# A hand-written TensorE order for the attentions of a second block: slots of one head and two query blocks, with pieces of projections between

## The chip, the cores and the metric

The kernel runs on one core of one Trainium2 chip. The metric is the device time of one execution in microseconds (us), the median over runs.

## The reference

Two blocks follow each other on a sequence of 512 tokens with 1024 features, in fp32. The first (a state-space branch and a windowed attention, then a feed-forward part) is left as it is. The change lies in the second block:

```python
z = rms_norm(x, g_norm) @ w_in
q, k, v, fl, gf, u, gs, qm, gm, gl = split_cols(z)
# forgetting attention: 12 heads of 64, causal, in 4 query blocks of 128
s = q.k/sqrt(64) + F_t - F_s          # F = cumsum(log_sigmoid(fl + b))
y_fox = softmax(s) @ v * silu(gf)
# S5: 48 groups of 16 channels, complex diagonal states; then gelu and a gated unit
y_s5 = gelu(s5_ssm(u)); y_s5 = y_s5 * sigmoid(y_s5 @ w_glu + b_glu) * silu(gs)
# memory attention: 4 heads of 128 over 256 memory keys
y_mem = softmax(qm.mk/sqrt(128)) @ mv * silu(gm)
merged = sum of sigmoid(gl_b) * (y_b @ w_proj_b) over the three branches
```

## The kernel before

Every projection is three products in a reduced fp32 format (hi times hi, hi times lo, lo times hi): `load_w` (L214) loads 512 KB of weights into `raw` (three buffers), ScalarE copies them to `whi` (L183) and VectorE writes the rest to `wlo` (L186); `whi` and `wlo` have two buffers each. `mm3` (L222) issues the three products of one 128-row slice, so a projection (`proj2`) is 24 matmuls of 512 columns into one of three PSUM banks, and a gated unit's second projection (`dense` on `w_glu`) 18.

The stretch that the change touches has ten units of work. Six are `fox(i)`, a pair of heads each: the projections of k, q and the gate; for each head the scores of query blocks 0 and 3 and then of 1 and 2 (tile `s`, two PSUM buffers), each with a row maximum (L782), its negative (L784), the exponential on ScalarE (tile `p`), a reciprocal (L795) and a scaling (L797), all in `softmax_rows`; then transposes of the scaled blocks on TensorE into the one PSUM bank of `pT`, five per two query blocks, in a group of four and a single one, each copied by ScalarE into `pt`; then 20 products with the values into `y`. Four are `mem(h)`, a memory head each. Beside them run the slots of S5 (`s5_slots`): per slot 8 products `px`, a scan and a dozen VectorE operations on them, 16 products `py`, a gelu, and small DMAs from GpSimd's queue (`ub`, `yp`). After S5 come six `glu(m)`, each the gate projection GS and the gated unit's projection.

A scheduling layer orders every engine's instructions: it simulates the program and, among instructions that are ready, takes the one of the highest priority, which follows the order of the text but for `tc.high_priority`. So TensorE's order is the scheduler's: single matmuls of projections of the next pairs stand between scores, transposes and S5 products. At run time each engine takes its instructions strictly in the order so fixed.

```python
ins[0]()
for x in range(10):
    if x < 9:
        ins[x + 1]()
    with tc.high_priority(offset=400):
        work[x]()
    next(s5_slot, None)
```

Of the kernel before, what the change touches and what calls it, by code (L numbers as in the profile page):

```python
# [8 lines left out]
F32 = mybir.dt.float32  # L9
# [8 lines left out]
P = 128  # L18
# [138 lines left out]
def emit(ctx, tc, A, out):  # L157
# [19 lines left out]
    set_banks(3)  # L177
    ctx.callback(lambda: banks["s"].close())

    V, S, G, T, DMA, QS = nc.vector, nc.scalar, nc.gpsimd, nc.tensor, nc.sync, nc.gpsimd  # L180
# [63 lines left out]
    def split(hi, lo, v):  # L244
        return act(hi, v, AF.Copy), tt(lo, v, f(hi), SUB)
# [1274 lines left out]
    def rtile(nm):  # L1520
        return qp.tile([P, L], F32, tag="r", name=nm, bufs=2)
# [38 lines left out]
    def fox_in(i):  # L1560
        a = proj2(U_K + i)
        kk = rtile("kk")
        act(kk, a, AF.Copy)
        kh = qp.tile([P, 2, L], F32R, tag="kh", name="kh", bufs=2)
        kl = kls[i % 2]
        for j in range(2):
            src = kk[64 * j:64 * j + 64]
            for q0 in (0, 64):
                act(kh[q0:q0 + 64, j], src, AF.Copy)
            tt(kl[64 * j:64 * j + 64, j], src, f(kh[64 * j:64 * j + 64, j]), SUB)  # L1570
        a = proj2(U_Q + i)
        r = rtile("r")
        act(r, a, AF.Copy, scale=0.125)
        f_in[i] = (kh, kl, split_heads(qp, r))

    def fox(i):
        kh, kl, qq = f_in.pop(i)
        pts = {}
        for hh in range(2):
            h = 2 * i + hh  # L1580
            lh = qp.tile([P, L], F32R, tag="lh", name="lh", bufs=2)
            h0, o0 = 64 * hh, 64 - 64 * hh
            G.tensor_copy(lh[h0:h0 + 64], qq[h0:h0 + 64, hh])
            V.tensor_scalar(lh[o0:o0 + 64], f(lf[o0:o0 + 64]), col("fsel", h)[o0:o0 + 64], None, op0=MUL)

            def score(n, hh=hh, lh=lh):
                sc = ps.tile([P, 512], F32, tag="s", name="s", bufs=2)
                w = max(256, (n + 1) * P)
                ql = qq[:, hh, n * P:(n + 1) * P]
                T.matmul(sc[:, 0:w], lhsT=ql, rhs=kh[:, hh, 0:w], start=True, stop=False)  # L1590
                T.matmul(sc[:, 0:w], lhsT=lh[:, n * P:(n + 1) * P], rhs=kl[:, hh, 0:w], start=False, stop=False)
                T.matmul(sc[:, n * P:(n + 1) * P], lhsT=identb, rhs=le_b, start=False, stop=True)  # L1592
                return sc[:, 0:(n + 1) * P]
            for ns in ((0, 3), (1, 2)):
                pr = softmax_rows([lambda n=n: score(n) for n in ns], None, qp, 512, 4)
                bl_ = [(n, kb) for n in ns for kb in range(n + 1)]
                pt = transposed([pr[ns.index(n)][:, kb * P:(kb + 1) * P] for n, kb in bl_], qp, 5, 4)
                for x, (n, kb) in enumerate(bl_):
                    pts[hh, n, kb] = pt[:, x]
        py = ps.tile([P, 512], F32, tag="y", name="y", bufs=1)  # L1600
        with tc.high_priority(offset=1000):
            for n in (2, 1, 3, 0):
                for kb in range(n, -1, -1):
                    for hh in (1, 0):
                        mm = T.matmul(py[64 * hh:64 * hh + 64, n * P:(n + 1) * P],
                                      lhsT=vx[:, kb, (2 * i + hh) * 64:(2 * i + hh) * 64 + 64],
                                      rhs=pts[hh, n, kb], start=(kb == n), stop=(kb == 0)).ins
                        in_order(mm, first=(n == 2 and kb == 2 and hh == 1))
        a = proj2(U_GF + i)
        s = rtile("sgf")  # L1610
        gate2(a, s)
        stt(yf[:, i], s, 0.5, py, MUL, MUL)


    ym = []

    def mem_in(h):
        a = proj2(U_QM + h)
        r = rtile("r")
        act(r, a, AF.Copy, scale=float(128.0 ** -0.5))  # L1620
        qq = qp.tile([P, 2, L], F32R, tag="qq", name="qm", bufs=2)
        split(qq[:, 0], qq[:, 1], r)
        f_in["m", h] = qq

    def mem(h):
        qq = f_in.pop(("m", h))
# [6 lines left out]
        pts = {}  # L1633
        for n2 in range(2):
            pr = softmax_rows([lambda n=n: score(n) for n in (2 * n2, 2 * n2 + 1)], None, qp, 512, 4)
            pt = transposed([pr[j][:, kb * P:(kb + 1) * P] for kb in range(2) for j in range(2)], qp, 5, 4)
            for kb in range(2):
                pts[n2, kb] = pt[:, 2 * kb:2 * kb + 2].rearrange("p a b -> p (a b)")
        py = ps.tile([P, 512], F32, tag="y", name="y", bufs=1)
        for n2 in range(2):  # L1640
            for kb in range(2):
                T.matmul(py[:, 256 * n2:256 * n2 + 256], lhsT=mvx[:, kb, h * P:(h + 1) * P], rhs=pts[n2, kb],
                         start=(kb == 0), stop=(kb == 1))
        a = proj2(U_GM + h)
        s = rtile("sgm")
        gate2(a, s)
        ym.append(pkv.tile([P, L], F32, tag=f"mk{h}", name=f"ym{h}"))
        stt(ym[h], s, 0.5, py, MUL, MUL)
# [32 lines left out]
    ins = [lambda i=i: fox_in(i) for i in range(6)] + [lambda h=h: mem_in(h) for h in range(4)]  # L1681
    work = [lambda i=i: fox(i) for i in range(6)] + [lambda h=h: mem(h) for h in range(4)]
    GLU = {5: (0,), 6: (1,), 7: (2, 3), 8: (4,), 9: (5,)}
    ins[0]()
    for x in range(10):
        if x < 9:
            ins[x + 1]()
        with tc.high_priority(offset=400):
            work[x]()
        next(s5_slot, None)  # L1690
        if x == 4:
            run(s5_slot)
            glu_in()
        for m in GLU.get(x, ()):
            glu(m)
# [134 lines left out]
```

## Time and profile before

| | |
|---|---|
| median of 3 runs | 2029.27 us (2028.99 to 2034.67) |
| the profiled execution's own time | 2029.36 us |
| its span on the core | 2027.6 us |
| TensorE busy | 1958.2 us, 97% of the span |
| VectorE busy | 1344.9 us, 66% |
| ScalarE busy | 967.5 us, 48% |
| chain that ended last | TensorE 89%, VectorE 5%, ScalarE 3% |

The span runs from the first instruction's start to the last one's end; the execution's own time has 1.8 us around it. Busy time of TensorE counts a matmul from issue to its modelled end, so a matmul of 512 columns has 0.39 us in the record although the next starts 0.23 us after it. PE is TensorE, DVE VectorE, ACT ScalarE, POOL GpSimd, SP the engine that issues the weights' DMAs.

### The profile page before, as it was taken

To read this page: it belongs to the slowest core of one execution; us is meant where nothing else is said; L and a number is where in the kernel's file an instruction comes from. 1 tells how busy PE (TensorE), PEld (TensorE's weight loads), DVE (VectorE), ACT (ScalarE), POOL (GpSimd) and SP (SyncE) were. 2 spreads that over 40 slices of the span, in tenths; PEclk is the share of its full clock that TensorE was granted. 3 is DMA by queue.
4 is the path that set the end of the run, shared out by engine and by line. 5 is a ranking of instruction groups with operands and counts; after the bars stand their busy time and mean duration, and the time that the engine had idled before them with its cause. 6 is when DMAs were issued, how large, how long until landed. Compare 5 with 4: busy or idle time off the path is not lost.

```text
span 2027.6 us, 29457 instructions
## 1 busy us (share of the span) xinstructions
PE 1958.2 (97%) x11312; PEld 1612.4 (80%) x11312; DVE 1344.9 (66%) x2375; ACT 967.5 (48%) x1825; POOL 214.2 (11%) x354
## 2 busy tenths in 40 slices
PE   6998999999999899999999999999999899999998
PEld 4787888888888777778777878878988677888887
DVE  6878877879567766457988885573587655524344
ACT  6745555454246665335433244554465644423233
POOL 2111111102020000001001210000532100000000
PEclk9998999999999999999999999999999999999999
DMA  7443545545322022343354643345764121333332
GB/s 297 116 146 125 158 140 178 182 129 170 94 63 63 22 84 88 100 125 110 116 169 128 218 145 97 105 123 167 193 178 130 47 66 58 135 96 88 104 97 90
DMA packets 84667, 250.48 MB, mean 124 GB/s; under 512 B 11632, under 2 KB 23280, under 8 KB 83760
## 3 DMA queue, kind: packets, MB, share of 16 engines
q1 hardware_dynamic: 67376, 199.45, 31.9%
q0 software_dynamic: 17152, 49.17, 7.8%
q8 instruction: 89, 1.46, 0.3%
q14 instruction: 50, 0.41, 0.1%
HBM read 228.78 MB, written 16.65 MB: 121 GB/s over the span
## 4 chain that ended last, share of the span: by engine, by line
PE 89%; DVE 5%; ACT 3%; DMA 1%; issue 1%; POOL 1%; SPq 0%; DVEq 0%; ACTq 0%; POOLq 0%
PE p L223 6%; PE p L225 6%; PE p L224 6%; PE pl L223 5%; PE pl L225 5%; PE pl L224 5%; PE po L223 3%; PE po L224 3%; PE po L225 3%; PE y L659 2%; PE pT L807 2%; PE ub L225 2%; PE pdn L225 2%; PE ua L225 2%; PE pdn L223 2%; PE ub L223 2%
## 5 line engine op out<-in xcount | busy, mean ns | idle before, releaser
L186 DVE TENSOR_TENSOR wlo<-raw,whi 128x1024 fp32r<-128x1024 f32 (+3 forms) x283 | 329.1, 1164 | 275.0 <-ACT whi L183 268.6
L183 ACT ACTIVATE whi<-raw 128x1024 fp32r<-128x1024 f32 (+3 forms) x283 | 282.8, 1001 | 445.3 <-PE p L224 135.0
L223 PE MATMUL pl<-hl,whi 128*128 128x512 f32 x528 | 212.5, 403 | 10.7 <-DVE cvc L189 8.2
L225 PE MATMUL pl<-hl,wlo 128*128 128x512 f32 x528 | 210.6, 399 | 1.0 <-DVE wlo L186 1.0
L224 PE MATMUL pl<-hl,whi 128*128 128x512 f32 x528 | 210.4, 398 | 0.0
L223 PE MATMUL p<-h,whi 128*128 128x512 f32 x504 | 200.2, 399 | 1.9 <-ACT uf L183 0.8
L225 PE MATMUL p<-h,wlo 128*128 128x512 f32 x504 | 199.7, 397 | 1.1 <-DVE wlo L186 1.1
L224 PE MATMUL p<-h,whi 128*128 128x512 f32 x504 | 199.6, 396 | 0.0
L223 PEld LDWEIGHTS pl<-hl,whi 128*128 128x128 f32 x528 | 100.8, 191 | 29.0 <-issue 10.4
L225 PEld LDWEIGHTS pl<-hl,wlo 128*128 128x128 f32 x528 | 100.6, 190 | 23.6 <-DVE wlo L186 1.7
L183 ACT ACTIVATE p<-s,nm 128x512 f32<-128x512 f32 (+4 forms) x128 | 80.1, 627 | 74.0 <-PE pT L807 34.2
L223 PEld LDWEIGHTS p<-h,whi 128*128 128x128 f32 x504 | 95.3, 189 | 22.9 <-ACT uf L183 1.2
L225 PEld LDWEIGHTS p<-h,wlo 128*128 128x128 f32 x504 | 95.1, 189 | 22.2 <-DVE wlo L186 2.0
L782 DVE TENSOR_REDUCE nm<-s 128x1 f32<-128x512 f32 (+4 forms) x128 | 76.6, 610 | 53.9 <-PE s L1592 28.7
L224 PEld LDWEIGHTS pl<-hl,whi 128*128 128x128 f32 x528 | 100.7, 191 | 13.8
L224 PEld LDWEIGHTS p<-h,whi 128*128 128x128 f32 x504 | 95.1, 189 | 20.1 <-DVE h L186 0.3
L183 ACT ACTIVATE pt<-pT 128x512 f32<-128x512 f32 (+1 forms) x152 | 70.7, 478 | 64.7 <-PE pT L807 52.8
L183 ACT ACTIVATE inj<-cs_t,dwt 128x128 f32<-128x128 f32 x256 | 80.9, 393 | 34.7 <-DVE es L635 27.7
L807 PE MATMUL pT<-cs_t,p 128*128 128x128 f32 x440 | 73.5, 281 | 9.9 <-ACT pt L183 9.6
L640 POOL DMA_DIRECT2D cf<-rows x64 | 34.7, 548 | 349.0 <-PE y L659 345.0
L225 PE MATMUL ua<-hf,wlo 128*128 128x512 f32 x176 | 69.4, 394 | 0.7 <-DVE wlo L186 0.7
L225 PE MATMUL ub<-hf,wlo 128*128 128x512 f32 x176 | 70.0, 398 | 0.0
(543 smaller groups left out, 4757.5 us busy)
## 6 DMA issues: line engine op xcount, KB each, us to landing
raw<-in_w_ta SPq DMA_DIRECT2D x66, 512.0 KB, 3.6
raw<-in_w_tb SPq DMA_DIRECT2D x63, 512.0 KB, 3.6
raw<-in_w_up SPq DMA_DIRECT2D x44, 512.0 KB, 3.6
es<-rows POOLq DMA_DIRECT2D x64, 256.0 KB, 5.7
cf<-rows POOLq DMA_DIRECT2D x64, 256.0 KB, 4.9
raw<-in_w_mod SPq DMA_DIRECT2D x32, 512.0 KB, 3.8
raw<-in_w_os SPq DMA_DIRECT2D x16, 512.0 KB, 3.8
raw<-in_w_out SPq DMA_DIRECT2D x16, 512.0 KB, 3.6
```

The costliest lines, as they stand in the source:

```text
L183: return S.activation(o, i, f, **kw)
L186: return eng.tensor_tensor(o, a, b, op=op)
L223: T.matmul(ps, lhsT=wh, rhs=ah, start=first, stop=False)
L224: T.matmul(ps, lhsT=wh, rhs=al, start=False, stop=False)
L225: T.matmul(ps, lhsT=wl, rhs=ah, start=False, stop=last)
L640: QS.dma_start(out=c_, in_=rows[r, 1].partition_broadcast(P))
L659: mm = T.matmul(py[64 * j:64 * j + 64, sl], lhsT=lt, rhs=rh, start=(step == 2), stop=(step == 0)).ins
L782: V.tensor_reduce(nm[:, j:j + 1], src, axis=AX.X, op=MAX)
L807: T.transpose(pt[:, j * P:(j + 1) * P], b, ident)
```

## The change

All products go through a class that, once switched on, ties each to the one before it, so that in this stretch TensorE's order is the order of the text. Projections are generators that yield after 12 of 24 matmuls. The text is a loop over pairs x, with four slots for a pair of heads and two for a memory head; a slot holds the scores of one head's two query blocks, four transposes of the slot before, 12 matmuls of a projection, the fifth transpose, and in some slots 12 more. Values and gate of a pair come a pair later. The order of the other engines is still the scheduler's. All counts of instructions, their shapes and all buffers stay.

```diff
+    class Products:
+        on, last = False, None
+        def put(self, r):
+            if self.on:
+                if self.last is not None:
+                    tc.add_manual_dep(r.ins, self.last.name, mybir.DependencyInfo(
+                        mybir.DependencyClass.NoSync, mybir.DependencyReason.DATA), reason="order")
+                self.last = r.ins
+            return r
...
+    def half_proj2(t, consume):
+        a = bank("p2")
+        hi, lo = load_w(flat(A["w_tb"][t]))
+        for k in range(KD):
+            ks = slice(k * P, (k + 1) * P)
+            mm3(a, hi[:, ks], lo[:, ks], acth[0](k), acth[1](k), k == 0, k == KD - 1)
+            if k == KD // 2 - 1:
+                yield
+        consume(a)
+        yield
...
     def glu(m):
-        a = proj2(U_GS + m)
-        gate2(a, s)
+        yield from half_proj2(U_GS + m, lambda a: gate2(a, s))
         pg = bank("pg")
         dense(flat(A["w_glu"][m]), 6, [act5], [pg])
...
+    run(fox_q(0))
+    run(fox_k(0))
+    T.on = True
+    for x in range(11):
+        slots = 4 if x < 6 else 2 if x < 10 else 1
+        qn = fox_q(x + 1) if x < 5 else mem_q(x - 5) if x < 9 else nothing()
+        kn = fox_k(x + 1) if x < 5 else nothing()
+        for s_ in range(slots):
+            if x < 6:
+                pr = fox_scores(x, s_ // 2, NS2[s_ % 2])
+            elif x < 10:
+                pr = mem_scores(x - 6, s_)
+            if s_ == 1:
...
+                    gate = gate_of(U_GF + x - 1 if x < 7 else U_GM + x - 7, o_, py_)
+            if turning:
+                step(turning)
+            if s_ == 0:
+                step(qn)
+            elif s_ == 1:
+                step(qn)
+            elif s_ == 2:
+                step(kn)
+            else:
+                step(gate)
+            if turning:
+                run(turning)
+            if x < 6:
+                if s_ == 1:
+                    step(kn)
...
+                elif s_ == 2:
+                    step(gate)
+            elif s_ == 1:
+                step(gate, 2)
+            else:
+                step(glus, 3)
+            if x < 10:
+                turning = turned(pr, pts_[x])
+            if x == 10:
+                step(glus, 6)
+        if x < 5:
+            fox_lh(2 * x + 2)
+            next(s5_slot, None)
+            if x == 4:
+                run(s5_slot)
+                glu_in()
+        if x == 5:
+            glus = (y for m in range(6) for y in glu(m))
+            step(glus, 3)
+        elif 5 < x < 10:
+            step(glus, 1 if x == 7 else 0)
```

**First pair, TensorE.** Before, from the S5 products `px` on: `p_13556` and `p_13596` are projections of the next pair, `s` the scores (L1590 to L1592).

```order
L1462 MATMUL px_13437<-ub,w_13270 128x64 x8
L225 MATMUL p_13556<-h_12445,wlo 128x512
L223 MATMUL p_13556<-h_12445,whi 128x512
L1590 MATMUL s<-kh,qq 128x256
L1590 MATMUL s<-kh,qq 128x512
L224 MATMUL p_13556<-h_12445,whi 128x512
L225 MATMUL p_13556<-h_12445,wlo 128x512
L223 MATMUL p_13556<-h_12445,whi 128x512
```

Now (every matmul carries the class's line, L195); `p_13583` is q of the next pair, of which 12 matmuls stand ahead of these rows, and `pT` are the transposes of the first slot's blocks:

```order
L195 MATMUL s<-kh,qq 128x256
L195 MATMUL s<-kl_12838,lh 128x256
L195 LDWEIGHTS cbf
L195 MATMUL s<-cbf 128x128
L195 MATMUL s<-kh,qq 128x384
L195 MATMUL s<-kl_12838,lh 128x384
L195 LDWEIGHTS cbf
L195 MATMUL s<-cbf 128x128
L198 MATMUL pT<-cs_t,p 128x128 x4
L195 MATMUL p_13583<-h_12445,whi 128x512 x2
```

Before, two projections and more of a third stood between the first scores and their completion; now the first slot's transposes come 12 matmuls and one slot's scores after them.

**First pair, VectorE.** Before, the work behind the first maxima (L782); `t_13822`, `uf` are the gelu of S5, `qq` a split of q:

```order
L186 TENSOR_TENSOR hs<-gr,xw_13455 128x8x64
L782 TENSOR_REDUCE nm<-s 128x1 x2
L186 TENSOR_TENSOR wlo<-raw,whi 128x1024
L186 TENSOR_TENSOR t_13822<-t_13822,yv 128x512
L784 TENSOR_SCALAR nm<-nm 128x1
L186 TENSOR_TENSOR qq<-r,qq 64x512
L784 TENSOR_SCALAR nm<-nm 128x1
L186 TENSOR_TENSOR qq<-r,qq 64x512
L189 SCALAR_TENSOR_TENSOR uf<-t_13822,yv 128x512
L795 RECIPROCAL sm<-sm 128x2
L797 TENSOR_SCALAR p<-p,sm 128x128
L797 TENSOR_SCALAR p<-p,sm 128x512
```

Now, up to the same two scalings (L817); the first maximum stands five rows further up, L802 is the maximum, L815 the reciprocal, `xr`, `xw` and `gr` (the scan) are S5's:

```order
L206 TENSOR_TENSOR xw<-xw,e_13271 128x512
L804 TENSOR_SCALAR nm<-nm 128x1
L206 TENSOR_TENSOR xr<-xr,xw 128x512
L802 TENSOR_REDUCE nm<-s 128x1
L1488 SCALAR_TENSOR_TENSOR gr<-e_13271,xr 128x512
L815 RECIPROCAL sm<-sm 128x2
L804 TENSOR_SCALAR nm<-nm 128x1
L1619 TENSOR_SCALAR lh<-lf,cols 64x512
L802 TENSOR_REDUCE nm<-s 128x1
L1461 COPY up<-uf 128x512
L817 TENSOR_SCALAR p<-p,sm 128x128
L817 TENSOR_SCALAR p<-p,sm 128x512
```

Before, the S5 operations up to `hs` lay ahead of the first maximum; now the S5 chain of that slot and the maxima of the next slot lie between the first maximum and the scalings.

**Gated units, ScalarE.** Before, `whi` of a gated unit (768 columns) stands with that of the gate ahead of it, six rows before the gate is used (`sg_15636`):

```order
L183 ACTIVATE whi<-raw 128x1024
L183 ACTIVATE whi<-raw 128x768
L183 ACTIVATE p,sm<-s,nm 128x128
L183 ACTIVATE pt<-pT 128x512
L183 ACTIVATE p,sm<-s,nm 128x512
L183 ACTIVATE pt<-pT 128x128
L183 ACTIVATE whi<-raw 128x1024
L183 ACTIVATE sg_15636<-p_15605 128x512
```

Now, for the gated unit m=1 (gate `p_15457`):

```order
L203 ACTIVATE p,sm<-s,nm 128x256 x2
L203 ACTIVATE pt<-pT 128x128
L203 ACTIVATE whi<-raw 128x768
L203 ACTIVATE sg_15456<-p_15457 128x512
L203 ACTIVATE whi<-raw 128x1024
L203 ACTIVATE t_15515<-pg,hb 128x512
```

The gated unit's `whi` now stands right ahead of the use of the gate's projection, with which it shares a buffer: a memory head's q projection is half done on TensorE and holds the other. In the built program two adjacent loads share their buffer in this way five times: m=1 behind its gate, m=2 behind its gate, m=3 behind its gate, the gate of m=4 behind m=3, and the gate of memory head 1 behind the q of memory head 3. Before, there is no such place.

## Rows read from the trace of the kernel before

**Rows 1.** The page: span, and busy time of each engine.

```profile
span 2027.6 us, 29457 instructions
PE 1958.2 (97%) x11312; PEld 1612.4 (80%) x11312; DVE 1344.9 (66%) x2375; ACT 967.5 (48%) x1825; POOL 214.2 (11%) x354
```

**Rows 2.** Busy time in three stretches: us, then PE, PEld, DVE, ACT, POOL, clock, DMA.

```profile
1450.00:1560.00 110.00, 110.00 (x651) 93.37 (x650) 87.12 (x163) 70.07 (x133) 40.05 (x71) 1.00 0.63 170
1560.00:1700.00 140.00, 128.86 (x793) 104.73 (x792) 81.52 (x189) 71.70 (x166) 10.12 (x13) 0.99 0.21 59
1700.00:1757.00 57.00, 57.00 (x276) 47.67 (x275) 29.36 (x61) 23.73 (x47) 0.00 (x0) 1.00 0.25 74
```

**Rows 3.** Who TensorE waited for, 1560 to 1700: us, times, longest.

```profile
PE pT L807 <- ACT pt L183: 6.7, 3, 2.8
PE y L1605 <- ACT pt L183: 2.2, 3, 1.1
```

**Rows 4.** Timeline of the longest wait: start, duration, engine, operation.

```profile
1577.08 2.56 ACT L183 ACTIVATE kh<-kk 64x512 fp32r<-64x512 f32 x4
...
1577.86 0.28 PE L807 MATMUL pT<-cs_t,p 128*128 128x128 f32 x1
...
1579.66 1.06 ACT L183 ACTIVATE whi<-raw 128x1024 fp32r<-128x1024 f32 x1
...
1580.62 0.26 ACT L183 ACTIVATE pt<-pT 128x128 f32<-128x128 f32 x1
...
1580.94 0.66 PE L807 MATMUL pT<-cs_t,p 128*128 128x128 f32 x4 [2.80 <-ACT pt L183]
```

**Rows 5.** Stretches around another wait, columns as in rows 2 (clock third from the end).

```profile
1606.00:1610.00 4.00, 1.44 (x10) 1.08 (x9) 2.91 (x8) 3.93 (x8) 0.82 (x1) 1.00 0.00 0
1610.00:1614.00 4.00, 4.00 (x13) 2.79 (x12) 3.24 (x8) 2.75 (x8) 0.00 (x0) 0.57 0.42 131
```

**Rows 6.** Timeline of TensorE: two projection matmuls, a pair's values; chain: S5's `px`.

```profile
1560.02 0.39 PE L224 MATMUL p<-h,whi 128*128 128x512 f32 x1
1560.25 0.39 PE L225 MATMUL p<-h,wlo 128*128 128x512 f32 x1
...
1565.05 2.40 PE L1605 MATMUL y<-pt,vx 128*64 128x128 f32 x40
...
1467.25 1.73 PE px L1462 x16
```

**Rows 7.** A stretch with S5 beside the attention, columns as in rows 2.

```profile
1500.00:1520.00 20.00, 20.00 (x115) 16.87 (x114) 17.46 (x37) 13.75 (x29) 7.01 (x13) 1.00 0.57 174
```

**Rows 8.** Timeline of VectorE: two operations, one behind the other.

```profile
1502.99 0.67 DVE L1441 COPY up<-uf 128x512 f32<-128x512 f32 x1
1503.59 1.14 DVE L189 SCALAR_TENSOR_TENSOR yv<-uf,cols,yp 128x512 f32<-128x512 f32 x1
```

**Rows 9.** Groups by line and form, 1450 to 1760: count, busy us, mean ns, idle before.

```profile
L186 DVE TENSOR_TENSOR wlo<-raw,whi 128x1024 fp32r<-128x1024 f32 x32 | 39.1, 1222 | 17.5 <-ACT whi L183 16.8 <-DMA w<-s5k 0.3
L183 ACT ACTIVATE whi<-raw 128x1024 fp32r<-128x1024 f32 x32 | 33.9, 1058 | 35.1 <-PE p L224 22.2 <-issue 9.5 <-PE pg L224 3.3
L186 DVE TENSOR_TENSOR wlo<-raw,whi 128x768 fp32r<-128x768 f32 x7 | 6.7, 953 | 7.8 <-ACT whi L183 7.8
L183 ACT ACTIVATE whi<-raw 128x768 fp32r<-128x768 f32 x7 | 5.9, 841 | 6.1 <-PE p L224 4.8 <-PE pg L224 1.3
L183 ACT ACTIVATE kh<-kk 64x512 fp32r<-64x512 f32 x24 | 15.1, 630 | 1.1 <-PE s L1590 0.8
L183 ACT ACTIVATE kk<-p 128x512 f32<-128x512 f32 x6 | 3.5, 590 | 0.0
L183 ACT ACTIVATE pt<-pT 128x512 f32<-128x512 f32 x32 | 19.1, 596 | 13.0 <-PE pT L807 13.0
L183 ACT ACTIVATE p<-s,nm 128x256 f32<-128x256 f32 x28 | 13.2, 472 | 29.7 <-PE pT L807 20.4 <-DVE nm L784 7.5 <-PE s L1592 1.5
```

More of the change, by code (lines that the diff above doesn't have):

```diff
@@ L178, in emit, with matmul, transpose @@
     ctx.callback(lambda: banks["s"].close())
-    V, S, G, T, DMA, QS = nc.vector, nc.scalar, nc.gpsimd, nc.tensor, nc.sync, nc.gpsimd
+    V, S, G, DMA, QS = nc.vector, nc.scalar, nc.gpsimd, nc.sync, nc.gpsimd
+    class Products:
[7 more added lines that the diff above has]
+            return r
+        def matmul(self, *a, **k):
+            return self.put(nc.tensor.matmul(*a, **k))
+        def transpose(self, *a, **k):
+            return self.put(nc.tensor.transpose(*a, **k))
+    T = Products()
     def act(o, i, f, **kw):
@@ L1558, in emit @@
     f_in = {}
[L1560 to L1599, printed above, removed]
-        py = ps.tile([P, 512], F32, tag="y", name="y", bufs=1)
[L1601 to L1610, printed above, removed]
-        gate2(a, s)
-        stt(yf[:, i], s, 0.5, py, MUL, MUL)
@@ L1615, in emit @@
-    ym = []
[L1617 to L1626, printed above, removed]
+    def half_proj2(t, consume):
[8 more added lines that the diff above has]
+        yield
@@ new lines, in fox_q, with consume, fox_k @@
+    def fox_q(i):
+        def consume(a):
+            r = rtile("r")
+            act(r, a, AF.Copy, scale=0.125)
+            f_in["q", i] = split_heads(qp, r)
+        return half_proj2(U_Q + i, consume)
+    def fox_k(i):
+        def consume(a):
+            kk = rtile("kk")
+            act(kk, a, AF.Copy)
+            kh = qp.tile([P, 2, L], F32R, tag="kh", name="kh", bufs=2)
+            kl = kls[i % 2]
+            for j in range(2):
+                src = kk[64 * j:64 * j + 64]
+                for q0 in (0, 64):
+                    act(kh[q0:q0 + 64, j], src, AF.Copy)
+                tt(kl[64 * j:64 * j + 64, j], src, f(kh[64 * j:64 * j + 64, j]), SUB)
+            f_in["k", i] = kh, kl
+        return half_proj2(U_K + i, consume)
@@ new lines, in turned @@
+    def turned(blocks, pts):
+        o = qp.tile([P, 5, P], F32, tag="pt", name="pt", bufs=4)
+        for x0 in range(0, len(blocks), 4):
+            pt = pst("pT")
+            bs = blocks[x0:x0 + 4]
+            for x, (key, b) in enumerate(bs):
+                T.transpose(pt[:, x * P:(x + 1) * P], b, ident)
+                pts[key] = o[:, x0 + x]
+            act(o[:, x0:x0 + len(bs)], v3(pt[:, 0:len(bs) * P], len(bs)), AF.Copy)
+            yield
+        pts["tile", blocks[0][0]] = o
@@ new lines, in fox_values, with gate_of, consume @@
+    def fox_values(i, pts):
+        py = ps.tile([P, 512], F32, tag="y", name="y", bufs=1)
+        for n in (0, 3, 1, 2):
+            for kb in range(n + 1):
+                for hh in range(2):
+                    T.matmul(py[64 * hh:64 * hh + 64, n * P:(n + 1) * P],
+                             lhsT=vx[:, kb, (2 * i + hh) * 64:(2 * i + hh) * 64 + 64],
+                             rhs=pts[hh, n, kb], start=(kb == 0), stop=(kb == n))
+        return py
+    def gate_of(t, o, py):
+        def consume(a):
+            s = rtile("sg")
+            gate2(a, s)
+            stt(o, s, 0.5, py, MUL, MUL)
+        return half_proj2(t, consume)
@@ L1628, in score, with mem_q, consume, mem_scores @@
+    ym = []
+    def mem_q(h):
+        def consume(a):
+            r = rtile("r")
+            act(r, a, AF.Copy, scale=float(128.0 ** -0.5))
+            qq = qp.tile([P, 2, L], F32R, tag="qq", name="qm", bufs=2)
+            split(qq[:, 0], qq[:, 1], r)
+            f_in["m", h] = qq
+        return half_proj2(U_QM + h, consume)
+    def mem_scores(h, n2):
+        qq = f_in["m", h]
         def score(n):
@@ L1632, in score, with mem_values @@
             return sc[:, 0:256]
[L1633 to L1638, printed above, removed]
+        pr = softmax_rows([lambda n=n: score(n) for n in (2 * n2, 2 * n2 + 1)], None, qp, 512, 4)
+        return [((n2, kb, j), pr[j][:, kb * P:(kb + 1) * P]) for kb in range(2) for j in range(2)]
+    def mem_values(h, pts):
         py = ps.tile([P, 512], F32, tag="y", name="y", bufs=1)
         for n2 in range(2):
+            o = pts["tile", (n2, 0, 0)]
             for kb in range(2):
[L1642 to L1648, printed above, removed]
+                T.matmul(py[:, 256 * n2:256 * n2 + 256], lhsT=mvx[:, kb, h * P:(h + 1) * P],
+                         rhs=o[:, 2 * kb:2 * kb + 2].rearrange("p a b -> p (a b)"), start=(kb == 0), stop=(kb == 1))
+        return py
     next(s5_slot, None)
@@ L1670, in glu @@
         act5 = (lambda k: g5["h"][:, k], lambda k: g5["l"][:, k])
-        a = proj2(U_GS + m)
         s = g5["p"].tile([P, L], F32, tag="sg5", name="sg5", bufs=2)
-        gate2(a, s)
+        yield from half_proj2(U_GS + m, lambda a: gate2(a, s))
         pg = bank("pg")
@@ L1679, in glu @@
         stt(uf[:, m], t, 0.125, s, MUL, MUL)
[L1681 to L1695, printed above, removed]
+        yield
@@ L1696, in emit @@
+    py_ = mem_values(3, pts_[9])
+    ym.append(pkv.tile([P, L], F32, tag="mk3", name="ym3"))
+    run(gate_of(U_GM + 3, ym[3], py_))
+    T.on = False
     glu_s.close()
```

39 lines of the change are left out of this document (added).

## The prediction, made before the run

> **What bounds the kernel now.** I began with the page's busy times: TensorE works 97% of the span and VectorE 66% [rows 1]. So time can only come from TensorE's idle time in the stretch that the change reorders, and be lost by new idle time there. The windows by stage say where it is: from 1450 to 1560 and from 1700 to 1757 TensorE is busy throughout; from 1560 to 1700 it is busy 128.86 of 140 us, so 11.1 us are lost [rows 2]. Then I asked who was waited for: the longest waits are three of TensorE's transposes (`pT`) for ScalarE's copy `pt`, 6.7 us, and three of the values for the same copies, 2.2 us [rows 3]. The timeline of one shows why [rows 4]: a single transpose ends near 1578.1, but ScalarE copies four `kh` (2.56 us) and a `whi` (1.06) ahead of its `pt`, and the next four transposes, which need the one bank, start 2.80 us late. At another such wait the granted clock falls: in 1606 to 1610 TensorE works 1.44 of 4 us, in 1610 to 1614 it is busy throughout at a mean granted clock of 0.57 [rows 5]. That stretch is mostly at the lower of the two levels (1.2 of 2.4 GHz), and 4 us at 0.57 lose 4 × 0.43 = 1.7 us. So the most that the new order can return is 11.1 + 1.7 = **12.8 us**.
>
> **What the change costs.** No instruction is added or removed, so TensorE's work is unchanged; the terms are waits. A matmul of 512 columns takes 0.23 us (start to start) [rows 6]. From a copy's end to the transposes that wait for it 0.06 us pass: `pt` ends at 1580.88, they start at 1580.94 [rows 4].
>
> *Start of the first pair.* k's second half must be copied and split before scores: `kk` 0.59, two `kh` 1.26 [rows 9], and one VectorE operation between 0.47 (the mean of 17.46 us over 37 instructions [rows 7]) and 1.14 [rows 8], taken as 0.68: 2.5 us. S5's `px` (1.73 [rows 6]) covers most. Cost 0.8; ends 0 and 2.5.
>
> *First pair, first slot.* From the first maximum to the second scaling 17 VectorE instructions stand in line, five more than the VectorE rows in the section on the change show; at 0.47 they are 8.0 us. TensorE has 12 projection matmuls (2.8) and about six scores of at most 384 columns, taken together as 1.2. Cost 8.0 − 4.0 = 4.0 before the transposes. Lower end 2.0, if a quarter of the 17 is done ahead; upper 7.4, at 0.67 each (the `up` of [rows 8]).
>
> *First pair, third slot.* The fifth transpose needs the bank back, whose copy stands on ScalarE behind the use of k's second half: `whi` 1.06, `kk` 0.59, `pt` 0.26 [rows 4], four `kh` 2.52, an exponential 0.47, `pt` 0.60, otherwise [rows 9], together 5.5 us; between them TensorE has six projection matmuls, 1.4, and, having no pair ahead, no gate. Cost 4.1; ends 1.6 (the four `kh` behind the copy) and 5.5.
>
> *Clock.* These waits are longer than the one behind which the clock fell [rows 5], so I take one fall, 1.7; ends 0 and 3.4. The Trainium skill, "TensorE: Matmul & The Clock Gate", section "HAM oscillation — how this bites in real kernels", says that a kernel that idles TensorE in each turn of its loop is throttled again each turn; the trace shows one fall among three such waits, and by that rule two or more would have to be counted, 3.4 us.
>
> *Second pair.* `py` and the next `px` share a bank, so TensorE waits for a copy between them, here costed by `pt`'s 0.60 [rows 9] and two signals, 0.7; its values wait behind one S5 operation on VectorE, 0.67 to 1.14 [rows 8], taken as 0.9; a transpose waits behind four ScalarE instructions of 13.75/29 = 0.47 [rows 7], 1.9. Sum 3.5. *Third and fourth:* 0.7 for the bank and 0.3 for the rest, 2.0 in both. *Fifth and sixth:* one transpose behind four `kh` and a `pt`, 2.52 + 0.60 = 3.1. These 8.6 are my least certain terms: ends half and one and a half times, 4.3 and 13.
>
> *Weights.* At five places two neighbouring loads use one `whi`/`wlo` buffer, and their matmuls stand directly behind each other, with nothing between. The new `whi` can only be written when the last reader of the old one ends: that matmul starts 0.46 before the next load's first would, and lasts 0.39 [rows 6], so 0.07 before. Then come `whi`, `wlo` and three signals, less two matmuls that need `whi` alone: for 768 columns 0.84 + 0.95 + 0.18 − 0.07 − 0.46 = 1.44, for 1024 1.06 + 1.22 + 0.18 − 0.53 = 1.93 (durations of [rows 9]). Three of the first and two of the second: 8.2. Ends 7.3 (no signals) and 10.6 (an instruction of 0.47 ahead each time). This term I trust most, as nothing covers it: behind the waiting matmul stands all that TensorE has left, and behind `whi` on ScalarE the sigmoid of the gate ahead, which can wait since its bank is one of three.
>
> *At nothing:* the weights' DMAs and POOL's, whose queues keep their order and load ahead into three `raw`; the DMA engines are busy 0.63 in the first stretch and 0.21 in the next [rows 2]. If they came late, `whi` would be the next thing waited for. VectorE and ScalarE have the same work; their queue is the rest of the story above.
>
> **Sum.** 0.8 + 4.0 + 4.1 + 1.7 + 3.5 + 2.0 + 3.1 + 8.2 = 27.4 us of new waits, less 12.8 = +14.6. The profiled execution took 2029.36 us (span 2027.6 and 1.8 around it), 0.1 from the median, so **2044 us**. With single ends this case runs from about 2035.5 to 2053; all ends at once give 2031 and 2059.
>
> **Rivals.**
> 1. *VectorE sets the pace in the first four pairs.* If its operations never overlap and the 17 of the first slot recur, two later pairs lose another 4.0 each: +8, 2052 us. For it: 17.46 of 20 us busy where S5 runs [rows 7]. Against: from 1450 to 1560 VectorE is busy 87.12 of 110 [rows 2], and the new text spreads S5 over more of TensorE's work; one S5 operation starts at 1503.59, 0.07 before the record of the one ahead ends [rows 8]. The Trainium skill, "VectorE: DVE Perf Modes", section "The DRAIN you can't avoid", says that a VectorE operation starts only when the pipe behind the one before it is empty; this case's row shows a start 0.07 early, and by the rule this rival would gain a little. Chance 0.18.
> 2. *Faster: the scheme does what its slots look made for.* ScalarE and VectorE have a slot of TensorE's work, 4 us and more, for each softmax, and get their part done inside it; then no transpose or value waits in any pair, the clock stays up, and the new waits are the weights' 7.3 and the start's 0.8. That is 8.1 − 12.8 = −4.7. If the orderly runs of scores also save what TensorE's mixed order loses beyond its waits, which no row here prices (an allowance of mine, 4 us), −8.7, 2021 us. It decides when the new waits stay below 12.8 − 6.1 = 6.7 us net of that saving. Against: four copies and one `whi` on ScalarE's queue already break the cover now [rows 4]. Chance 0.10.
> 3. *No change.* The first pair's softmax is done in time (no 4.0, 4.1, 1.7), the middle terms come at half (4.3), weights and start as costed: 0.8 + 4.3 + 8.2 = 13.3, less 12.8: +0.5, 2030 us. Chance 0.15.
> That the change does nothing is excluded: the printed order of TensorE differs through the whole stretch, and it is strict.
>
> **How the numbers follow.** A measurement of this kernel can tell about 0.3%, 6.1 us: below 2023.3 is faster, above 2035.4 slower. My case has 0.57 and rival 1 0.18, both slower: 0.75. Rival 3 gives 0.15 for no change, rival 2 0.10 for faster. The range 2027 to 2057 takes in rival 3, my case and rival 1, and leaves out rival 2 and the far tail of all ends.
>
> **What would show it.** Right: in the first 30 us of the stretch two waits of about 4 us at `pT`, for VectorE's scaling and ScalarE's copy; behind them a clock slice under 1.00; five waits of projection or gated-unit matmuls for `whi` and `wlo`, of 1.4 to 1.9 us, where before there are none after 1700 [rows 2]; the stretch ends some 14 us later than at 1757. Wrong: a full TensorE from 1450 on, `pT` waits below 1 us, or a stretch that ends before 1757; if the five weight waits alone are missing, my neighbouring-buffer term is wrong, and the time is about 2036.

## The result, and the profile after

The changed kernel takes 2051.68 us (median of 4 runs, 2050.22 to 2053.59) against 2030.34 for the kernel before on the same chip: a ratio of 1.0103, with a 95% interval of 1.0089 to 1.0117. It is slower by 21 us. The profiled execution took 2050.64 us; its span is 2048.8 us, where it was 2027.6 [rows 1]. The page of the kernel after, span and busy time:

```profile
span 2048.8 us, 29457 instructions
PE 1967.6 (96%) x11312; PEld 1619.1 (79%) x11312; DVE 1344.1 (66%) x2375; ACT 967.9 (47%) x1825; POOL 211.8 (10%) x354
```

VectorE and ScalarE do the same work as before. TensorE is busy for 9.4 us more (1958.2 to 1967.6) and not busy for 11.8 us more (69.4 to 81.2). Together that is the 21.2 us of the span.

The span of a single execution is not a clean measure of the change, though. TensorE issues 11312 matmuls in either kernel, up to the 8001st and from the 10301st on the same ones in the same order. By their start times in the traces, the part ahead took 1385.5 us before and 1380.7 after, the stretch between the two 403.1 and 429.1, and what follows, to the last matmul's start, 231.9 in both. So the stretch grew by 26.0 us, and 4.8 of these don't show in the span, since the part ahead, whose work is the same, went faster in this execution. In the kernel before the clock fell there at 689 and at 822 us, for 3.4 us each time, and in the kernel after it did not, which is a part of it. That is luck; how the executions that were not profiled divide is not shown. Over the eleven profiles of this document the part ahead took from 1380.7 to 1388.9 us, so single spans that differ by a few microseconds say little, and effects are read below from the stretch and from the median times.

The windows of the three stretches that answer to [rows 2] (columns: PE, PEld, DVE, ACT, POOL, granted clock, DMA share, GB/s) say where:

```profile
1435.00:1580.00 145.00, 134.19 (x797) 114.41 (x797) 97.85 (x197) 80.28 (x164) 41.45 (x74) 0.88 0.50 131
1580.00:1721.00 141.00, 134.18 (x753) 109.06 (x751) 78.42 (x172) 69.87 (x150) 7.48 (x12) 1.00 0.23 66
1721.00:1778.00 57.00, 53.86 (x249) 43.77 (x249) 23.74 (x45) 19.54 (x36) 0.00 (x0) 1.00 0.25 74
```

Two things are new. TensorE is idle in the first and the last stretch, where it was full before from 1450 to 1560 and from 1700 to 1757 [rows 2]; over the three stretches 20.8 us are lost, of 343 (before, 11.8 from 1435 to 1757). And the first stretch runs at a mean granted clock of 0.88, where 1450 to 1560 had 1.00 [rows 2]. Who TensorE waits for from 1440 to 1790 (total, times, longest), to be read against [rows 3]:

```profile
PE pT L198 <- ACT pt L203: 7.0, 6, 2.9
PE pT L198 <- DVE p L817: 2.6, 1, 2.6
PE pg L195 <- ACT whi L203: 2.2, 3, 0.7
PE px L195 <- ACT yb L203: 2.1, 3, 0.7
PE p L195 <- ACT whi L203: 1.8, 2, 0.9
PE p L195 <- DVE wlo L206: 1.7, 3, 0.6
PE s L195 <- ACT kh L203: 1.0, 1, 1.0
...
PE pg L195 <- DVE wlo L206: 0.8, 3, 0.3
```

The old wait of transposes for `pt` is as large as before (6.7 then, 7.0 now), and the waits for VectorE's scaling, for S5's `yb` and for `whi` and `wlo` have come on top.

**First pair.** The timeline of VectorE, from the first maximum to the scalings, and of the transposes that wait:

```profile
1462.52 0.29 DVE L802 TENSOR_REDUCE nm<-s 128x1 f32<-128x128 f32 x1 [0.61 <-PE s L195]
...
1466.88 1.21 DVE L1488 TENSOR_TENSOR_SCAN gr<-e,xr 128x512 f32<-128x512 f32 x1
...
1469.88 0.67 DVE L817 TENSOR_SCALAR p<-p,sm 128x128 f32<-128x128 f32 x2
1470.21 1.09 PE L198 MATMUL pT<-cs_t,p 128*128 128x128 f32 x3 [2.63 <-DVE p L817]
```

S5's scan stands in the softmax of the first slot, which takes VectorE from 1462.52 until the scalings at 1469.88, and the transposes start 2.63 us late. In the third slot the fifth transpose waits for its bank, whose copy stands behind four `kh` and an exponential on ScalarE:

```profile
1483.51 2.55 ACT L203 ACTIVATE kh<-kk 64x512 fp32r<-64x512 f32 x4
...
1486.55 0.59 ACT L203 ACTIVATE pt<-pT 128x512 f32<-128x512 f32 x1
...
1487.19 0.47 PE L198 MATMUL pT<-cs_t,p 128*128 128x128 f32 x1 [2.86 <-ACT pt L203]
```

**Clock.** Windows of the same columns around the waits:

```profile
1468.00:1470.00 2.00, 0.00 (x0) 0.00 (x0) 1.90 (x7) 1.82 (x4) 0.00 (x0) 0.96 0.02 6
1470.00:1472.00 2.00, 1.79 (x6) 1.48 (x7) 2.00 (x5) 0.45 (x1) 1.44 (x3) 0.50 0.06 16
1486.00:1488.00 2.00, 0.81 (x5) 0.81 (x5) 1.22 (x4) 1.95 (x7) 0.00 (x0) 0.73 0.70 174
1488.00:1502.00 14.00, 13.31 (x58) 12.33 (x59) 3.12 (x9) 2.83 (x6) 4.19 (x8) 0.50 0.57 139
1530.00:1532.00 2.00, 1.36 (x9) 1.36 (x10) 0.00 (x0) 0.58 (x1) 1.12 (x3) 0.82 0.82 299
1532.00:1538.00 6.00, 6.00 (x24) 5.00 (x24) 2.91 (x7) 2.71 (x6) 3.06 (x6) 0.50 1.00 210
```

The clock falls to its lower level four times: in the first pair's waits at 1470 and 1487, and then at 1531 and (the same picture) at 1565, where TensorE had waited only 0.69 us. The timeline shows that wait, of S5's `px` for the copy of `py` out of the bank that both use:

```profile
1529.56 0.39 PE L195 MATMUL py<-ub,w 128*128 128x64 f32 x2
...
1529.99 0.60 ACT L203 ACTIVATE yb<-py 128x512 f32<-128x512 f32 x1 [2.15 <-PE py L195]
...
1530.64 2.68 PE L195 MATMUL px<-ub,w 128*128 128x64 f32 x14 [0.69 <-ACT yb L203]
```

Added up over the stretch, the clock is at the lower level for 34.1 us (3.4, 17.1, 6.8 and 6.8), against 3.4 us before. What such a microsecond costs can be read from two projection matmuls inside the second fall:

```profile
1502.01 0.63 PE L195 MATMUL p<-h,wlo 128*128 128x512 f32 x1
1502.44 1.05 PE L195 MATMUL p<-h,whi 128*128 128x512 f32 x2
```

From start to start they are 0.43 us apart, at full clock 0.23 [rows 6]. So a microsecond at the lower level in which TensorE has work loses 0.20/0.43 = 0.47 us. 1.3 of the 34.1 us were idle anyway.

**Weights.** One of the five places, the gated unit m=1:

```profile
1666.02 0.40 PE L195 MATMUL p<-h,wlo 128*128 128x512 f32 x1
1666.27 0.84 ACT L203 ACTIVATE whi<-raw 128x768 fp32r<-128x768 f32 x1 [5.05 <-PE p L195]
...
1667.14 0.96 DVE L206 TENSOR_TENSOR wlo<-raw,whi 128x768 fp32r<-128x768 f32 x1 [5.92 <-ACT whi L203]
...
1667.16 0.50 PE L195 MATMUL pg<-g5h,whi 128*128 128x512 f32 x1 [0.75 <-ACT whi L203]
...
1668.16 0.50 PE L195 MATMUL pg<-g5h,wlo 128*128 128x512 f32 x1 [0.26 <-DVE wlo L206]
```

ScalarE had been idle for 5.05 us when `whi` started, and what ended that was TensorE's last `p`, not a DMA: the buffer had not been free. The waits stand at 1666, 1693 and 1719 (0.71 to 0.75 and 0.26 us) and at 1725 and 1735 (0.92 and 0.53).

### The profile page after: what moved, and what is told of

Its sections match the earlier page's. It is cut to its first block, busy times and chain, and to the rows that moved or that the text cites. A ratio compares the mean times of both kernels' runs of the same rounds, so it can differ in the third digit from the quotient of the medians.

```text
span 2048.8 us, 29457 instructions
## 1 busy us (share of the span) xinstructions
PE 1967.6 (96%) x11312; PEld 1619.1 (79%) x11312; DVE 1344.1 (66%) x2375; ACT 967.9 (47%) x1825; POOL 211.8 (10%) x354
## 4 chain that ended last, share of the span: by engine, by line
PE 84%; DVE 5%; ACT 4%; DMA 3%; issue 3%; POOL 1%; SPq 0%; DVEq 0%; ACTq 0%; POOLq 0%
PE p L195 15%; PE pl L195 15%; PE po L195 10%; PE ub L195 6%; PE ua L195 6%; PE pdn L195 5%; PE y L195 5%; PE pp L195 4%; PE s L195 3%; PE pv L195 3%; PE pc L195 2%; PE pT L198 2%; PE st L195 2%; PE mod L195 1%; DVE wlo L206 1%
## 5 line engine op out<-in xcount | busy, mean ns | idle before, releaser
L195 PE MATMUL pl<-hl,whi 128*128 128x512 f32 x1056 | 338.7, 400 | 10.6 <-DVE cvc L209 8.2
L195 PE MATMUL p<-h,whi 128*128 128x512 f32 x1008 | 323.7, 401 | 3.8 <-ACT whi L203 2.5
L195 PEld LDWEIGHTS p<-h,whi 128*128 128x128 f32 x1008 | 188.3, 191 | 45.4 <-ACT whi L203 4.4
L195 PEld LDWEIGHTS pl<-hl,whi 128*128 128x128 f32 x1056 | 188.3, 191 | 42.5 <-issue 10.4
L195 PE MATMUL pl<-hl,wlo 128*128 128x512 f32 x528 | 210.6, 399 | 0.7 <-DVE wlo L206 0.7
L195 PE MATMUL p<-h,wlo 128*128 128x512 f32 x504 | 199.7, 396 | 2.2 <-DVE wlo L206 2.2
L195 PEld LDWEIGHTS pl<-hl,wlo 128*128 128x128 f32 x528 | 100.4, 190 | 23.3 <-DVE wlo L206 1.4
L802 DVE TENSOR_REDUCE nm<-s 128x1 f32<-128x512 f32 (+4 forms) x128 | 76.6, 611 | 64.3 <-PE s L195 63.4
L195 PEld LDWEIGHTS p<-h,wlo 128*128 128x128 f32 x504 | 95.8, 190 | 25.3 <-DVE wlo L206 3.9
L195 PE MATMUL ua<-hf,whi 128*128 128x512 f32 x352 | 110.3, 391 | 0.5 <-DVE hf L206 0.5
L195 PE MATMUL ub<-hf,whi 128*128 128x512 f32 x352 | 110.1, 391 | 0.0
L203 ACT ACTIVATE p<-s,nm 128x512 f32<-128x512 f32 (+4 forms) x128 | 79.9, 626 | 53.6 <-DVE nm L804 25.7
L195 PEld LDWEIGHTS ub<-hf,whi 128*128 128x128 f32 x352 | 65.8, 188 | 14.6 <-issue 1.2
L195 PEld LDWEIGHTS ua<-hf,whi 128*128 128x128 f32 x352 | 65.8, 188 | 14.5 <-DVE hf L206 0.9
L195 PEld LDWEIGHTS pc<-hc,whi 128*128 128x128 f32 x352 | 65.3, 193 | 14.5 <-DVE cv L209 1.9
L195 PE MATMUL pc<-hc,whi 128*128 128x256 f32 x352 | 72.3, 288 | 1.2 <-DVE cv L209 1.2
L198 PEld LDWEIGHTS pT<-cs_t,p 128*128 128x128 f32 x440 | 51.6, 144 | 25.3 <-ACT pt L203 13.8
```

Of the source, the lines that this page charges most:

```text
L195: return self.put(nc.tensor.matmul(*a, **k))
L198: return self.put(nc.tensor.transpose(*a, **k))
L802: V.tensor_reduce(nm[:, j:j + 1], src, axis=AX.X, op=MAX)
```

## The experiments

Each kernel was compared with the kernel before on the same chip. The theory was that three separate things make the 21 us: waits of the first pair for want of cover, shared weight buffers, and a clock that falls at S5's products. The main rival was that VectorE or ScalarE sets the pace, so that a wait taken away comes back elsewhere. Only one execution of each kernel was profiled. Its part ahead, its stretch, and the stretch's idle time between TensorE's records and time at the lower clock level (us, taken from the traces as above):

| kernel | ahead | stretch | idle | lower clock |
|---|---|---|---|---|
| before | 1385.5 | 403.1 | 12.1 | 3.4 |
| after | 1380.7 | 429.1 | 22.0 | 34.1 |
| `e1_apart` | 1383.4 | 422.2 | 21.9 | 17.1 |
| `e2_px_bank` | 1386.6 | 421.0 | 20.6 | 23.9 |
| `e3_whole_q` | 1383.3 | 420.6 | 15.8 | 34.1 |
| `e5_v_pieces` | 1384.8 | 417.0 | 15.6 | 23.9 |
| `e6_all` | 1385.7 | 398.8 | 8.8 | 3.4 |
| `e7_all_spread` | 1381.8 | 398.8 | 8.7 | 3.4 |
| `e8_py_early` | 1388.9 | 397.3 | 8.0 | 0 |
| `e10_two` | 1384.8 | 401.4 | 9.7 | 10.2 |
| `e9_two_bank` | 1386.6 | 393.3 | 6.1 | 0 |

**px moved off py** (`e1_apart`). The slot of S5 is cut behind `py`, and its second half comes in the next pair's first slot:

```diff
             for lag, fn in ((3, s5_gelu), (2, s5_y), (1, s5_state), (0, s5_in)):
                 if 0 <= k - lag < 6:
                     fn(k - lag)
+                if lag == 2:
+                    yield
             yield
...
+            if s_ == 0 and 0 < x < 5:
+                next(s5_slot, None)
             if turning:
                 run(turning)
```

> S5's products px are moved off py, twelve projection matmuls, six scores and four transposes behind it, in pairs 1 to 3; nothing else moves on TensorE. Theory A (the block of 24 small S5 products with a wait of 0.69 us in it makes the clock fall at 1531 and 1565, and prolongs the fall of 1487): the three waits of px for yb (2.1 us together) and the two falls of 6.5 us go, at 0.3 to 0.5 us lost per us of low clock 2 to 3 us each, so 6 to 8 us faster than the changed kernel, about 2045, and the fall of 1487 shorter by another 1 to 4 us. Theory B (the long waits of the first pair alone bring the clock down and S5's products, wherever they stand, do so too): only the 2.1 us of the waits go, about 2049.5, and the falls stay in the pairs 2 and 3.

Measured: 2047.76 us, ratio 1.0087 (1.0074 to 1.0100), span 2044.6. The windows at the two places, now with no fall:

```profile
1528.00:1538.00 10.00, 10.00 (x76) 9.09 (x74) 5.53 (x14) 4.46 (x12) 4.37 (x8) 1.00 0.65 150
1560.00:1570.00 10.00, 10.00 (x77) 9.14 (x76) 5.53 (x14) 4.46 (x12) 4.37 (x8) 1.00 0.63 162
```

Both falls are gone, and 17.1 us at the lower level are left, in the first pair and at the `py` behind it. `px`'s waits are gone too, but six of 0.36 to 0.41 us at scores and transposes have taken their place, so the idle time between TensorE's records is the same (22.0 and 21.9 us). With that the stretch measures the clock: 17.0 us less at the lower level made it 6.9 us shorter, about 0.41 for each, near the 0.47 of the two matmuls. The span is only 4.2 us shorter, as the part ahead took 2.7 more in this execution, so the 0.25 that the expectation for `e6_all` takes from this run was a misreading. The stretch gained the 6 to 8 us expected, but from the clock alone; the time of 2045 was not reached.

**px in a bank of its own** (`e2_px_bank`):

```diff
-        px5 = p5t("px5")
+        px5 = bank("px5")
```

> px goes into one of the three banks of the projections in place of the one that it shares with py, so it needs not wait for the copy of py; it still stands right behind py, 24 small products in a row. If the wait of 0.69 us is what tips the clock, the falls at 1531 and 1565 go as well as the waits: 6 to 8 us faster than the changed kernel, about 2045. If the row of small products is enough for it, the clock falls there as before and only 2.1 us of waits go, about 2049.5. A new wait of a projection for its bank would show as p waiting for ScalarE or VectorE, at most 1 us each time.

Measured: 2048.31 us, ratio 1.0088 (1.0075 to 1.0101). At the places of the two falls, where `py` and `px` still stand in a row:

```profile
1532.00:1540.00 8.00, 8.00 (x66) 7.42 (x65) 4.96 (x11) 4.44 (x9) 3.11 (x7) 1.00 0.51 160
1562.00:1570.00 8.00, 8.00 (x66) 7.43 (x65) 5.05 (x12) 4.44 (x9) 3.14 (x7) 1.00 0.52 154
```

So the row of small products does not lower the clock by itself. The stretch is 8.1 us shorter, though the edit also moved the order ahead of the first pair: `px` came up to stand behind `py` at 1435, waited there 2.6 us for the DMA of `ub`, and the clock fell behind that (6.8 us). The first pair's falls stayed (3.4 and 13.7 us). The time is 3.4 us shorter, half of the 6 to 8 expected, and the part ahead took 5.9 us more in the profiled execution.

**The memory heads' q whole** (`e3_whole_q`):

```diff
             if s_ == 0:
-                step(qn)
+                step(qn, 2 if x > 5 else 1)
             elif s_ == 1:
-                step(qn)
+                step(qn if x < 6 else gate)
...
             elif s_ == 1:
-                step(gate, 2)
+                step(gate)
```

> In the memory heads' part the q projection is done whole in the first slot and the gate's halves take its place in the second, so no two neighbouring loads share a whi/wlo buffer. Theory A (the buffers are the cause of the five waits at 1666, 1693, 1719, 1725 and 1735, 0.75+0.26 three times and 0.92+0.53 two times, 5.9 us): all five are gone, 5.9 us faster than the changed kernel, about 2045.8, with the clock's falls unchanged. Rival (ScalarE's queue would be late with whi in any case): waits for whi and wlo stay at other places, under 2 us gained.

Measured: 2044.56 us, ratio 1.0071 (1.0058 to 1.0085), span 2042.9. In its waits no `pg` and no `whi` is left before 1760, only one `wlo` of 0.6 that stands ahead of the first pair in both kernels. The idle time from about 1430 on falls from 21.3 to 15.4 us, by 5.9 as expected, and the low clock is unchanged (34.1 us). The stretch is 8.5 us shorter, the time 7.1. The theory holds; some of the rest is the way in which waits are counted, which comes below.

**Cover in the first pair** (`e5_v_pieces`). The value projection `fox_v(2)` yields after each of its four groups of 24 matmuls, and in pair 0 the pieces are dealt out anew:

```diff
+    vn = fox_v(2)
+    next(vn)
...
-            if s_ == 0:
+            if x == 0:
+                step(vn if s_ < 2 else qn if s_ == 2 else kn, 2 if s_ == 0 else 1)
+            elif s_ == 0:
                 step(qn)
...
-            if x < 6:
+            if x == 0:
+                step(qn if s_ == 1 else kn, 1 if s_ in (1, 2) else 0)
+            elif x < 6:
```

> The last third of the value projection (96 matmuls of 256 columns) is cut into four pieces and put into the first pair as cover: one ahead of the first scores, two behind them, one in the second slot; the next pair's q and k come one place later. Theory A (the first pair lacks cover, as it has no pair ahead whose values and gate could stand in it): its waits of 0.99, 0.70, 2.63, 0.67 and 2.86 us, 7.85 together, fall below 2, and the clock falls at 1470 (3.4 us) and 1487 (16.5 us) go or the second becomes one of 6.5 behind S5's products, so 9 to 13 us faster than the changed kernel, 2039 to 2043. Rival (VectorE and ScalarE are the bound there, and the waits only move): the waits stay above 5 us in the sum of the first two pairs, 0 to 3 us gained.

Measured: 2040.32 us, ratio 1.0050 (1.0036 to 1.0063). None of the first pair's five waits is left but one of 0.3 us. Behind the pair a new one came, of `px` for `yb`, 2.5 us, since four `kh` now stand ahead of `yb` on ScalarE, and the clock fell there for 10.2 us, and for 6.8 us at each of the next two pairs' `px`. Theory A holds; the rival had allowed 3 us at most, and the time fell by 11.4 and the stretch by 12.1.

**All three** (`e6_all`): the edits of `e1_apart`, `e3_whole_q` and `e5_v_pieces`.

> All three edits in one: px twelve projection matmuls behind py, the memory heads' q whole, the value projection's last third as cover in the first pair. If the causes add, the changed kernel's span of 2048.8 us loses 5.9 (weights), 7.85 (first pair) and all 34.1 us of low clock at 0.25 us each (what e1_apart gave: 17 us less of it, 4.2 us of span, the idle time the same), 8.5; px's waits are exchanged for those of e1_apart between 1522 and 1557: 2026.5 of span, about 2028, no difference from the kernel before that can be told. Rival (VectorE sets the pace of the pairs, so the waits move on): the idle time from 1440 to 1780 stays above 15 us, and the time above 2036.

Measured: 2024.33 us, ratio 0.9963 (0.9951 to 0.9975), faster than the kernel before. Of the idle time from about 1430 on 8.1 us are left, where taking away the weights' 5.9 and the first pair's 7.85 would leave 7.5, and one fall of 3.4 us. So the causes add, and the time is below the 2028 expected because that sum went by 0.25 for a microsecond at the lower level: the stretch is 30.3 us shorter, 13.2 by idle time, and 30.7 us of the lower level went. The rival, that the waits only move, wanted more than 15 us of idle time and is out.

**g5h dealt out** (`e7_all_spread`), and **py earlier** (`e8_py_early`), both on top of `e6_all`:

```diff
             stt(g5["l"][:, q], uf[:, q], 0.5, f(g5["h"][:, q]), MUL, SUB)
+            if q % 2:
+                yield
...
+            if x == 5 and s_ < 3:
+                next(g5_in, None)
```

> As e6_all, and the six copies g5h with their differences g5l are made two by two in the slots of the sixth pair, in place of all at its start. If they are what ScalarE's copies pt wait behind at 1611 to 1631 (1.92, 0.80, 0.56, 0.70 us), these go: 4.0 us less than e6_all, about 2024. If not, the waits stay, the same as e6_all.

Measured: 2026.14 us, ratio 0.9972 (0.9962 to 0.9982); a miss. The waits of 1.92, 0.56, 0.56 and 0.70 us are the same: the scheduler still puts a `whi`, two `g5h` and the copy `kk` ahead of the `pt` that TensorE needs.

```diff
             if turning:
                 step(turning)
+            if s_ == 3 and x < 5:
+                next(s5_slot, None)
...
-            if s_ == 0 and 0 < x < 5:
-                next(s5_slot, None)
```

> As e7_all_spread, but py moves ahead by twelve projection matmuls and a transpose into the fourth slot, and px stays at the end of the pair, so VectorE's work on px does not run into the next pair's softmax. If that collision makes e1_apart's waits of 0.36 to 0.41 us (six in two pairs, 2.3 us), they go: about 2022, faster than the kernel before by 0.3 to 0.5%. If they come from elsewhere, the same as e7_all_spread.

Measured: 2025.12 us, ratio 0.9963 (0.9949 to 0.9976); a miss. The six waits of about 0.4 us went, but the transposes came to wait for VectorE's scaling by 0.52, 1.24 and 0.73 us in the same pairs.

**The clock once more, without the first pair's waits** (`e10_two`, `e9_two_bank`). `e10_two` is `e6_all` with `px` back behind `py`; `e9_two_bank` differs from it in one line:

```diff
-        px5 = p5t("px5")
+        px5 = (bank if T.on else p5t)("px5")
```

> e6_all without the move of px: q whole and the value pieces only, px right behind py in the bank they share. Expected by the sum: e5_v_pieces (2040.3) less the 5.9 us of the weights, 2034.5; px waits at three places (2.53, 0.69, 0.69 us in e5_v_pieces) and behind each the clock falls, some 24 us at the lower level in all. If q whole or something else in e6_all, and not px's place, took the falls away, there are none here and the time is 2028 or less.

Measured: 2031.17 us, ratio 1.0004 (0.9992 to 1.0017), between the 2034.5 of the sum and the 2028 of the other case, with 12 runs from 2026.44 to 2035.12. The kernel before has as wide a range on this chip, 2025.26 to 2034.84 in 17 runs. The clock goes with it: the three runs of `e10_two` below 2027 us had a mean granted clock of 0.989 to 0.991, the six above 2032 one of 0.986 to 0.988. The profiled execution was one of the short ones, 2026.96 us. Its waits of `px`, and the windows at the three places (same columns as above):

```profile
PE px L195 <- ACT yb L203: 3.9, 3, 2.5
```

```profile
1486.00:1494.00 8.00, 6.46 (x28) 5.80 (x29) 2.42 (x6) 3.23 (x8) 3.92 (x8) 0.57 1.02 222
1520.00:1528.00 8.00, 7.31 (x50) 6.21 (x49) 4.60 (x10) 3.78 (x9) 4.18 (x8) 1.00 0.98 217
1551.00:1559.00 8.00, 7.31 (x50) 6.11 (x48) 4.60 (x12) 3.78 (x9) 4.18 (x8) 1.00 0.98 225
```

Behind the wait of 2.5 us the clock fell; behind the two of 0.69 us it stayed up this time, where `e5_v_pieces` with the same waits in the same order had a fall at each.

> As e10_two, but within the ordered stretch px has a bank of the projections for itself, so that it stands right behind py and waits for nothing; the row of 24 small S5 products is as in e10_two. Theory A (the wait between py and px tips the clock): no fall from 1440 to 1580, and the time of e6_all, 2024, or 1 to 2 us less. Theory B (the row of small products holds it down, and the first pair's waits had hidden this in e2_px_bank): the clock falls at two or three of the rows, and the time is 2029 to 2033.

Measured: 2017.81 us (6 runs, 2015.50 to 2023.79), ratio 0.9937 (0.9920 to 0.9954): the fastest of all, and below the 2022 to 2024 that theory A gave. Its waits from 1435 to 1760 and the first and second stretch:

```profile
PE pT L198 <- ACT pt L203: 3.2, 3, 1.9
PE pT L198 <- DVE nm L803: 0.8, 1, 0.8
PE pv L195 <- DVE wlo L206: 0.5, 1, 0.5
PE s L195 <- DVE kl L206: 0.3, 1, 0.3
```

```profile
1435.00:1580.00 145.00, 144.20 (x971) 124.59 (x971) 113.64 (x234) 94.86 (x198) 48.97 (x87) 1.00 0.57 154
1580.00:1705.00 125.00, 120.91 (x673) 99.58 (x672) 67.07 (x143) 58.45 (x123) 3.70 (x6) 1.00 0.24 68
```

TensorE is busy 144.2 of the first 145 us at full clock, with all rows of small products in place; VectorE works 113.6 of those, so it could follow. Against `e10_two`, whose matmuls come in the same order, the stretch is 8.1 us shorter: the 3.9 us of `px`'s waits and the fall behind the first of them are gone. What is left is 4.1 us in the last pairs, mostly for `pt` copies that still wait in ScalarE's queue.

## Why the prediction was right, and where its sum was off

The measured 2051.68 us lie in the range, and the sign and the kind of the costs were right. The forecast of 2044 was 8 us low. For the stretch itself, forecast at +14.6, it was 11.4 low; luck in the part ahead of the profiled execution hid 4.8 of that in the span. Term by term, with the idle time between TensorE's records of the kernel after:

| term | forecast, us | measured, us |
|---|---|---|
| start of the first pair | 0.8 | 0.99 |
| first slot | 4.0 | 0.70 + 2.63 = 3.33 |
| third slot | 4.1 | 0.67 + 2.86 = 3.53 |
| second pair | 3.5 | 0.69 + 0.29 = 0.98 |
| third and fourth | 2.0 | 0.69 + 0.69 = 1.38 |
| fifth and sixth | 3.1 | 1.92 + 0.13 + 0.80 + 0.56 + 0.69 = 4.10 |
| weights | 8.2 | 3 × 1.01 + 2 × 1.44 = 5.9 |
| clock | 1.7 | 34.1 us at the lower level, about 15 |

*Waits.* They were forecast at 25.7 us and the records show 20.2. Part of this is how they are counted: the forecast counted from when the next matmul would have started, 0.23 us after the last, the record from its modelled end, 0.39. For the weights of m=1 the count by starts is 1667.16 − 1666.25 = 0.91 and 1668.16 − 1667.73 = 0.43, together 1.34 against the forecast's 1.44. With these 0.16 us for each of the 24 waits the measured sum comes to about 24.0, close to the forecast. The term that was too large is the second pair's: its values and its transpose hardly waited.

*What the order returns.* The 12.8 us of the old waits and the old fall were counted as wholly returned. That was right: none of them is at its old place, and what `pt` still costs (7.0 us) is in the new terms. But the 11.1 us of waits in it were counted by the record and the new ones by starts; by starts the eleven old waits were 12.9.

*The clock is the term that failed.* "I take one fall, 1.7" had the price of a fall right and their number wrong: there were four falls, the second of them prolonged from the fifth transpose through `py` and `px`. With 0.47 us lost for each of the 32.8 us at the lower level in which TensorE was not idle, the kernel after loses 15.4 us to the clock and the kernel before, with 3.4, 1.6: about 14 us, where the forecast had 1.7 for 1.7 and so nothing. With the waits, 24.0 less 12.9, and 1.2 us more of waits outside the table, the sum is 26 us, which is what the stretch grew by. So the clock is the larger half of the cost and the reason why the forecast was low. I had seen the bank that `py` and `px` share, costed its wait at 0.7 (measured 0.69), and not asked what a wait at that place does to the clock. The Trainium skill, "TensorE: Matmul & The Clock Gate", section "HAM oscillation — how this bites in real kernels", says a kernel that idles TensorE in each turn of its loop is throttled again in each turn; I had weighed it against the one fall of [rows 5] and kept the one. The trace after agrees with the page for the first three pairs: two falls in the first, and one behind each of the second and the third. It doesn't for the later ones, whose waits of up to 1.92 us brought none.

*Rival 1 had the time, 2052, and not the cause.* It wanted two later pairs to lose 4 us each to VectorE; they lose 0.29 us to transposes, and in `e9_two_bank` VectorE follows a full TensorE. A forecast that is hit by a rival's number is checked by its place in the trace, not by the number.

*Rival 2* was right that the scheme can be faster than the scheduler's order. `e9_two_bank` gains 0.6% with the same slots, but only after three things that the change had lacked: cover in the first pair, weights that alternate, and no wait inside S5's products.

*At nothing* held for the weights' DMAs: none of the five late `whi` had waited for `raw`. Four had waited for TensorE, and for the one at 1693 the profile names nothing.

## What to carry to other kernels

When an order is written by hand, follow each pool through it as well as each engine: two neighbouring loads in one buffer cost 1.0 to 1.4 us of waiting for `whi` and `wlo` at each of five places here, and another order of the same matmuls removed them all. The first turn of a loop has no turn ahead from which to borrow cover; give it independent work (here a projection that is needed only later). A short wait can cost more by the clock than by itself: behind 0.69 us came 6.8 us at the lower level, which at 0.47 are some 3 us. So give the second user a bank of its own, and price falls by the number of places at which they may come. And before a difference of two profiles is put down to an edit, compare the parts that the edit left alone.

## What had not been expected

The clock fell behind a wait of only 0.69 us, twice in the kernel after, between 16 and 8 products of 64 columns; with the wait taken out and the same row of products left in place it stayed up (`e2_px_bank`, `e9_two_bank`). The fall does not come every time: `e10_two` has the same two waits and no fall in its profiled execution, and its longer runs had a lower clock. Whether they had the falls at these places is not shown, as none of them was profiled, and what decides it in the single case is open. The part ahead of the stretch shows the same chance: with the same work the clock fell at about 820 us in nine of the eleven profiles and not in two.

In the kernel before, one wait of 2.56 us brought a fall [rows 5] and the longer one of 2.80 did not [rows 4]; in the kernel after, one of 1.92 us at 1619 brought none, while the same 1.92 us in `e6_all`, `e7_all_spread` and `e10_two` is followed by 3.4 us at the lower level. So the length of a wait alone doesn't tell.
